# Where the sums of the down weights are made, and two small moves around the output projection, in a decoder layer on one core

## The chip, the cores and the metric

One Trainium2 chip, and one core of it. The metric is the device time of one execution of the whole layer in microseconds (us); lower is better. Several runs of a kernel are given as a median with the lowest and the highest. Engines are named as the profile names them: PE is the matrix engine (PEld its weight loads), DVE the vector engine, ACT the scalar engine, POOL the GpSimd engine. SP is the engine whose queue issues the DMA transfers of this kernel.

## The reference

One layer of a decoder with 1024 tokens of 1024 float32 values: one projection, two attention branches (a forgetting attention, and a sparse one that keeps 256 keys per query), a gated mix, and a SwiGLU feed-forward block, each of the last two behind a layer norm. Cut to what matters here:

```python
proj = x @ w_in[l]
(fq, fk, fv, f_logit, dq, dk, dv, iq, ik, iw, g_a, g_b) = _split_columns(proj)
o_a = _fox_attention(...)
o_b = _dsa_attention(...)
merged = (jax.nn.sigmoid(g_a) * (o_a @ w_branch_a[l])
          + jax.nn.sigmoid(g_b) * (o_b @ w_branch_b[l]))
x = _layer_norm(ALPHA * x + merged @ w_out[l], ln1_g[l], ln1_b[l])
gate, up = jnp.split(x @ w_ffn_in[l], 2, axis=-1)
ffn = (jax.nn.silu(gate) * up) @ w_ffn_out[l]
x = _layer_norm(ALPHA * x + ffn, ln2_g[l], ln2_b[l])
```

The feed-forward block is 1024 to 2 x 2816 and back to 1024.

## The kernel before, in words

Every float32 product is made of three matmuls on a high and a low part of each operand (`mm3`, lines 97 to 101): a weight tile is loaded, ACT copies it rounded (the high part), and POOL or DVE subtracts that from the original (the low part). PE cannot begin a product before its high part is there (line 99), nor go on past the first matmul before its low part is there (line 100).

The stages in order of time:

1. Projections and attention (to about 800 us). Between them PE works off "filler" projections, the last of which are the gates (`gate`, line 374): a product in a PSUM bank, a tanh on ACT (line 380), a write to DRAM (line 381). The PSUM pool of this stage is closed after the last gate, and the next stage takes its banks.
2. Branch projections (line 637 on). For each half of the tokens and each of four column groups, two branches: `load_wb` splits a branch weight (ACT line 631, POOL line 632 the first half of the low part, DVE line 633 the second half), PE makes two products of 12 matmuls each (24 in all), DVE folds the gate in. The buffers of the high and low parts are two deep. `load_wb` runs at raised priority. In the same loop, eight weights of the output projection are loaded and split: ACT line 671, POOL line 672, one instruction for all 1024 columns.
3. Output projection, layer norm and transposes (about 890 to 1022 us).
4. The up stage of the feed-forward block (line 829 on), 22 steps of 128 gate and 128 up columns. The products are made by Strassen's scheme (Winograd's form): seven products of 12 matmuls a step (five in the first three steps, whose other two were made ahead). For a step c, a gate weight `wraw` and an up weight `wup` are loaded, DVE makes four sums of them (lines 838 to 841, tiles `ss`), ACT and POOL split the seven into tiles `w` (lines 789 and 790), ten of which are in a ring. PE fills PSUM banks `pb`, eight deep; DVE empties each by adding it to running sums `u` and `h` (lines 806 and 858), ACT and DVE finish the gated product (lines 864, 866, 867).
5. The same step also prepares the weights of the next stage: a tile `wb` with four 128x256 blocks of `w_ffn_out` is loaded by two transfers (line 875), four sums are made in place (lines 877 to 880), each is written to a DRAM buffer `abd` (line 882). The other half of `abd` are the blocks of the gated product (line 889) and their sums (891 to 896).
6. The down stage (about 1465 us to the end) reads `abd` back and makes the seven products of 2816 to 1024.

The order on each engine is set at build time. PE's order in the stages 3 to 6 is written out by hand; the other engines' instructions are placed by a scheduler that takes, by priority, what its own model of the chip finds ready. Priority follows program order, and `high_priority(offset=HURRY)` raises it. A tile's buffer comes from a pool by its tag; a new tile of the tag waits until an old one is no longer used. So the scheduler starts a load as soon as its tag has a free buffer. Before the change:

```python
up = ffl.tile([128, 1024], F32, name="wup", tag="wup", bufs=2)
wb = ffl.tile([128, 4, 256], F32, name="wb", tag="wb", bufs=1)
```

The tag `wb` is used by the sums alone: as soon as the four writes of one step have landed, the tile of the next step is loaded, whatever step PE is at. Each engine, and SP's queue, works strictly in the order given to it: an instruction that waits holds up all behind it.

Of the kernel before, what the change touches and what calls it, by code (L numbers as in the profile page):

```python
# [8 lines left out]
F32 = mybir.dt.float32  # L9
# [3 lines left out]
AF = mybir.ActivationFunctionType  # L13
OP = mybir.AluOpType
# [24 lines left out]
AHEAD, LASTC, HURRY = 3, 8, 100  # L39
# [10 lines left out]
def trunk_kernel(ctx: ExitStack, tc: tile.TileContext, xT, xn, wt, wbr, wout, wfi, wfo,  # L50
                 lnp, bf, alq, alk, out):
    nc = tc.nc
    te, dve, act, pool, sp = nc.tensor, nc.vector, nc.scalar, nc.gpsimd, nc.sync
# [14 lines left out]
    def f(ap):  # L68
        return ap.bitcast(F32)
# [16 lines left out]
    def load_w(src, hi=None, lo=None):  # L86
        raw = wp.tile([128, 1024], F32, name="wraw", tag="wraw", bufs=2)
        sp.dma_start(raw, src)
        if hi is None:
            hi = wp.tile([128, 1024], F32R, name="whi", tag="whi", bufs=2)  # L90
            lo = wp.tile([128, 1024], F32R, name="wlo", tag="wlo", bufs=2)
        act.activation(hi, raw, AF.Copy)  # L92
        pool.tensor_tensor(lo, raw, f(hi), op=OP.subtract)  # L93
        return hi, lo
# [21 lines left out]
    def ps_mm():  # L116
        return psA.tile([128, 512], F32, name="mm", tag="mm", bufs=NMM)
# [52 lines left out]
    for h in range(2):  # L170
        s = slice(h * 512, h * 512 + 512)
        ps = ps_mm()
# [69 lines left out]
    for c in range(4):  # L242
        w = split_w(raw0, pool) if c == 0 else load_w(wt[C_IQ + c])
        iq = [idx.tile([128, 768], F32R, name="iq", tag="iq", bufs=4) for _ in range(2)]
        for q, (half, c0, n, d0) in enumerate(((0, 256, 256, 0), (1, 0, 512, 256))):
            ps = ps_mm()
# [6 lines left out]
        for a in range(2):  # L253
            h = 2 * c + a
            for i in range(2, 8):
                n = 128 * (i + 1)
# [109 lines left out]
    def proj_steps(ps, w, half):  # L366

        hi, lo = w
        for k in range(KT):
            mm3(ps, [(hi[:, k * 128:k * 128 + 128], lo[:, k * 128:k * 128 + 128],  # L370
                      XH[half][:, k], XL[half][:, k])], k == 0, k == KT - 1)
            yield

    def gate(br, c):
        w = load_w(wt[(C_GA, C_GB)[br] + c])
        for h in range(2):
            ps = ps_mm()
            yield from proj_steps(ps, w, h)
            g = at.tile([128, 512], F32, name="g", tag="g", bufs=2)
            act.activation(g, ps, AF.Tanh, scale=0.5)  # L380
            sp.dma_start(gdr[br][c, :, h * 512:h * 512 + 512], g)

    def project(br, pr, made):
# [220 lines left out]
    def ps_b():  # L604
        return psB.tile([128, 512], F32, name="ob", tag="ob", bufs=4)
# [6 lines left out]
    WOH, WOL = [], []  # L612
# [3 lines left out]
    def load_raw_b(src, shape):  # L616
        raw = bp.tile(shape, F32, name="braw", tag="braw", bufs=2)
        sp.dma_start(raw, src)
        return raw

    def load_o(o, br, s):

        for k in range(0, 4, 2):
            raw = load_raw_b(odr[br][k:k + 2, :, s].rearrange("k p t -> p k t"), [128, 2, 512])
            act.activation(o[:, 0, k:k + 2], raw, AF.Copy)
            dve.tensor_tensor(o[:, 1, k:k + 2], raw, f(o[:, 0, k:k + 2]), op=OP.subtract)
# [11 lines left out]
    for h in (1, 0):  # L638
        s = slice(h * 512, h * 512 + 512)
        if h:  # L640
            O = [xm.tile([128, 2, 4, 512], F32R, name=f"oh{br}", tag="x", bufs=4) for br in range(2)]
        else:
            O = [bp.tile([128, 2, 4, 512], F32R, name=f"ol{br}") for br in range(2)]
        MH[h] = xm.tile([128, KT, 512], F32R, name=f"mh{h}", tag="x", bufs=4)
        ML[h] = xm.tile([128, KT, 512], F32R, name=f"ml{h}", tag="x", bufs=4)
        load_o(O[0], 0, s)
        load_o(O[1], 1, s)
        for c2 in (range(4) if h else range(3, -1, -1)):
            m = []
            for br in range(2):  # L650
                if h or c2 < 3:
                    with tc.high_priority(offset=HURRY):
                        WB[br] = load_wb(br, c2)
                wh, wl = WB[br]
                for x in range(2):
                    c = 2 * c2 + x
                    g = bp.tile([128, 512], F32, name="g", tag="g", bufs=7)
                    sp.dma_start(g, gdr[br][c, :, s])
                    ps = ps_b()
                    mm3(ps, [(wh[:, b0:b0 + 128], wl[:, b0:b0 + 128], O[br][:, 0, k], O[br][:, 1, k])  # L660
                             for k, b0 in enumerate(range(x * 512, x * 512 + 512, 128))])
                    dve.scalar_tensor_tensor(g, g, 1.0, ps, op0=OP.add, op1=OP.mult)
                    m.append(g)
                    if br:
                        dve.tensor_tensor(g, g, m[x], op=OP.add)
                        act.activation(MH[h][:, c], g, AF.Copy, scale=0.5)
                        dve.scalar_tensor_tensor(ML[h][:, c], g, 0.5, f(MH[h][:, c]),
                                                 op0=OP.mult, op1=OP.subtract)
            k = c2 + 4 * (1 - h)
            raw = load_raw_b(wout[k * 128:k * 128 + 128], [128, 1024])  # L670
            act.activation(WOH[k], raw, AF.Copy)
            pool.tensor_tensor(WOL[k], raw, f(WOH[k]), op=OP.subtract)
    _bp.close()


# [76 lines left out]
    for t in range(NB):  # L752
        half, c0 = divmod(TOK[t] * 128, 512)
        bs = fin.tile([128, 2, 6], F32, name="bs", tag="bs", bufs=2)
        for n in range(2):
            ns = slice(n * 512, n * 512 + 512)
            ps = ps_b()
# [54 lines left out]
    for c in range(AHEAD):  # L812
        raw = load_raw(wfi[c])
# [9 lines left out]
    def ps_c():  # L823
        return psC.tile([128, 512], F32, name="pb", tag="pb", bufs=8)

    ffl, _ffl = open_pool("ffl")
    ring[0:0] = [(ffl, "wt0", 1)]
    ring += [(ffl, f"wt{k}", 1) for k in range(1, 4)]
    for c in range(FC):
        g = load_raw(wfi[c])  # L830
        up = ffl.tile([128, 1024], F32, name="wup", tag="wup", bufs=2)
        sp.dma_start(up, wfi[FC + c])
        g1_, g2_, u1_, u2_ = g[:, 0:512], g[:, 512:1024], up[:, 0:512], up[:, 512:1024]
        new = c >= len(ahead)
        a11, a12 = (slot(), slot()) if new else (None, None)
        s2, s3, s1, s4, a22 = (slot() for _ in range(5))
        r1, r2, r3, r4 = (ffl.tile([128, 512], F32, name="ss", tag="ss", bufs=4) for _ in range(4))
        dve.tensor_tensor(r1, u1_, u2_, op=OP.add)
        dve.tensor_tensor(r2, r1, g1_, op=OP.subtract)
        dve.tensor_tensor(r3, g1_, u1_, op=OP.subtract)  # L840
        dve.tensor_tensor(r4, g2_, r2, op=OP.subtract)
        if new:
            split(a11, g1_)
            split(a12, g2_)
        split(s2, r2)
        split(s3, r3)
        split(s1, r1)
        split(s4, r4)
        split(a22, u2_)
        u = c11(ps_c, (a11, a12)) if new else ahead[c]  # L850
        h = ffl.tile([128, 2, 512], F32, name="h", tag="h", bufs=3)
        U, sg, h0, h1 = u[:, 0], u[:, 1], h[:, 0], h[:, 1]

        def add(to, w, x, *more):
            ps = ps_c()
            product(ps, w, x)
            for o, i in ((to, to), *more) if to is not None else more:
                dve.tensor_tensor(o, ps, i, op=OP.add)  # L858

        add(U, s2, T2)  # L860
        add(None, s3, T3, (h0, U))
        add(None, s1, T1, (h1, h0), (U, U))
        add(U, s4, B22)
        act.activation(U, U, AF.Silu)
        add(h0, a22, T4)
        dve.tensor_tensor(h1, h1, U, op=OP.mult)
        dve.tensor_tensor(h0, h0, sg, op=OP.mult)


        j, x = divmod(c, 2)  # L870
        cols = slice(x * 256, x * 256 + 256)
        wb = ffl.tile([128, 4, 256], F32, name="wb", tag="wb", bufs=1)
        for y in range(2):
            rows = wfo[(2 * j + y) * 128:(2 * j + y + 1) * 128]
            sp.dma_start(wb[:, 2 * y:2 * y + 2], rows.rearrange("p (a n) -> p a n", a=2)[:, :, cols])
        b11, b12, b21, b22 = (wb[:, y] for y in range(4))
        dve.tensor_tensor(b11, b12, b11, op=OP.subtract)  # L877
        dve.tensor_tensor(b12, b22, b12, op=OP.subtract)  # L878
        dve.tensor_tensor(b22, b22, b11, op=OP.subtract)  # L879
        dve.tensor_tensor(b21, b21, b22, op=OP.subtract)  # L880
        for p, b in ((5, b11), (7, b12), (6, b22), (4, b21)):
            sp.dma_start(abd[p][j][:, 1, cols], b)
        if x == 0:
            even, even_u = h, U
            continue

        a11, a21, a12, a22 = even[:, 0], even[:, 1], h0, h1
        for p, a in ((1, a11), (2, a12), (4, a22)):
            sp.dma_start(abd[p][j][:, 0], a)
        q2, q3, q4 = U, sg, even_u  # L890
        dve.tensor_tensor(q3, a11, a21, op=OP.subtract)
        dve.tensor_tensor(a21, a21, a22, op=OP.add)
        dve.tensor_tensor(q2, a21, a11, op=OP.subtract)
        dve.tensor_tensor(q4, a12, q2, op=OP.subtract)
        for p, a in ((7, q3), (5, a21), (6, q2), (3, q4)):
            sp.dma_start(abd[p][j][:, 0], a)
# [166 lines left out]
```

## Time and profile before

| | us |
|---|---|
| median of 3 runs (lowest, highest) | 1687.06 (1686.71, 1687.7) |
| the profiled execution, its own time | 1685.55 |
| its span, first to last instruction | 1683.6 |
| PE busy | 1611.2 |
| DVE busy | 1186.1 |
| ACT busy | 777.3 |
| POOL busy | 673.3 |

All times of the trace are counted from the start of the span. A PE busy time is modelled and matmuls overlap, so a PE that is "busy" can still be slow; how fast it goes is read from the number of matmuls in a window. The granted clock is a share of 2.4 GHz. "Idle before, releaser" is the time an engine stood still before an instruction, and what ended that.

### The profile page before, as it was taken

The numbers are of one execution on the slowest core, as the hardware profiler recorded it, in microseconds if no ns is written. First come the engines' busy times: TensorE is split into PE (matmuls) and PEld (weight loads), VectorE is DVE, ScalarE is ACT, GpSimd is POOL, SyncE is SP. The second block draws the span as 40 slices with busy tenths as digits, with TensorE's granted clock in tenths as the row PEclk, the third lists the DMA queues.
The fourth block names the chain that finished last, engine by engine and source line by source line (L and its number), as shares of the span: only waits on it lengthen the run. The fifth ranks groups of instructions, "written<-read, shape, count | busy, mean of one in ns | idle before, by whom it ended". The sixth has DMA issues, their size and how long they took to land. (4 is left out here: it accounts for less than half of the span.)

```text
span 1683.6 us, 22519 instructions
## 1 busy us (share of the span) xinstructions
PE 1611.2 (96%) x7722; PEld 1314.1 (78%) x7722; DVE 1186.1 (70%) x2074; ACT 777.3 (46%) x1374; POOL 673.3 (40%) x652
## 2 busy tenths in 40 slices
PE   7998999998999999999999999999899999999997
PEld 5776887776788888888778877877677888888886
DVE  5889999979645454544775569776778766567776
ACT  6777878884444445544431034222123333253341
POOL 1122333332333333332441136434345555377673
PEclk9999999999999999999999999999899999999999
DMA  5112212121122222223865123565554333398552
GB/s 176 48 40 65 60 45 59 57 70 43 57 66 63 70 58 71 61 65 126 270 208 194 50 88 102 190 203 184 172 180 139 107 101 107 132 329 309 179 169 105
DMA packets 96379, 202.83 MB, mean 120 GB/s; under 512 B 10820, under 2 KB 37444, under 8 KB 96264
## 3 DMA queue, kind: packets, MB, share of 16 engines
q1 hardware_dynamic: 96264, 201.39, 36.6%
q8 instruction: 61, 1.00, 0.3%
q14 instruction: 54, 0.44, 0.1%
HBM read 139.40 MB, written 53.03 MB: 114 GB/s over the span
## 5 line engine op out<-in xcount | busy, mean ns | idle before, releaser
L99 PE MATMUL mm<-xh,whi 128*128 128x512 f32 (+1 forms) x720 | 296.0, 411 | 16.2 <-ACT whi L147 6.4
L101 PE MATMUL mm<-xl,whi 128*128 128x512 f32 (+1 forms) x720 | 281.4, 391 | 1.1 <-DVE xl L157 1.0
L100 PE MATMUL mm<-xh,wlo 128*128 128x512 f32 (+1 forms) x720 | 280.7, 390 | 0.5 <-DVE wlo L148 0.5
L479 POOL TENSOR_SCALAR p<-p,st 128x512 f32<-128x512 f32 (+1 forms) x192 | 113.8, 601 | 321.5 <-DVE st L476 268.8
L790 POOL TENSOR_TENSOR w<-ss,w 128x512 fp32r<-128x512 f32 x88 | 129.4, 1487 | 207.5 <-ACT w L789 188.8
L93 POOL TENSOR_TENSOR wlo<-wraw,whi 128x1024 fp32r<-128x1024 f32 x43 | 103.5, 2406 | 164.4 <-ACT whi L92 143.1
L99 PEld LDWEIGHTS mm<-xh,whi 128*128 128x128 f32 x720 | 136.8, 190 | 31.1 <-issue 6.4
L101 PEld LDWEIGHTS mm<-xl,whi 128*128 128x128 f32 x720 | 136.0, 189 | 32.0 <-DVE xl L157 2.3
L100 PEld LDWEIGHTS mm<-xh,wlo 128*128 128x128 f32 x720 | 136.8, 190 | 12.8 <-DVE wlo L148 1.0
L504 DVE TENSOR_TENSOR pl<-T,ph 128x512 fp32r<-128x512 f32 (+1 forms) x160 | 100.6, 634 | 36.6 <-ACT ph L503 34.7
L100 PE MATMUL acc<-fs 128*128 128x512 f32 x308 | 120.0, 389 | 0.6 <-DVE fs L930 0.6
L101 PE MATMUL acc<-fs 128*128 128x512 f32 x308 | 119.9, 389 | 0.0
L99 PE MATMUL acc<-fs 128*128 128x512 f32 x308 | 119.8, 389 | 0.0
L503 ACT ACTIVATE ph<-T 128x512 fp32r<-128x512 f32 (+1 forms) x160 | 87.3, 552 | 38.8 <-PE T L502 36.1
L310 ACT ACTIVATE junk<-sm,nt 128x1024 bf16<-128x1024 f32 (+2 forms) x93 | 96.8, 1041 | 14.6 <-DVE nt L318 12.8
L502 PE MATMUL T<-identf,p 128*128 128x128 f32 x576 | 90.6, 273 | 4.1 <-POOL p L479 2.0
L931 POOL TENSOR_TENSOR fs<-fraw,fs 128x512 fp32r<-128x512 f32 x47 | 81.1, 1740 | 26.9 <-ACT fs L929 23.1
L502 PEld LDWEIGHTS T<-identf,p 128*128 128x128 f32 x576 | 71.2, 140 | 26.1 <-DVE pl L504 4.1
L512 PE MATMUL O<-pl,V 128*128 128x256 f32 x320 | 82.3, 281 | 1.3 <-DVE pl L504 1.3
L511 PE MATMUL O<-ph,V 128*128 128x256 f32 x320 | 83.3, 282 | 0.0
L99 PE MATMUL pb<-x1h,w 128*128 128x512 f32 x176 | 72.0, 409 | 10.5 <-DVE h L858 9.3
L930 DVE TENSOR_TENSOR fs<-fraw,fs 128x512 fp32r<-128x512 f32 x47 | 57.0, 1225 | 31.1 <-ACT fs L929 31.1
(284 smaller groups left out, 4167.6 us busy)
## 6 DMA issues: line engine op xcount, KB each, us to landing
wraw<-in_wt_dram SPq DMA_DIRECT2D x45, 512.0 KB
fraw<-abd SPq DMA_DIRECT2D x30, 512.0 KB
wraw<-in_wfi_dram SPq DMA_DIRECT2D x25, 512.0 KB
wup<-in_wfi_dram SPq DMA_DIRECT2D x22, 512.0 KB
wb<-in_wfo_dram SPq DMA_DIRECT2D x44, 256.0 KB
abd<-wb SPq DMA_DIRECT2D x88, 128.0 KB
abd<-h SPq DMA_DIRECT2D x44, 256.0 KB
abd<-u SPq DMA_DIRECT2D x33, 256.0 KB
```

Source lines behind the costliest of these rows:

```text
L93: pool.tensor_tensor(lo, raw, f(hi), op=OP.subtract)
L99: te.matmul(ps, ah, bh, start=(first and i == 0), stop=False)
L100: te.matmul(ps, al, bh, start=False, stop=False)
L101: te.matmul(ps, ah, bl, start=False, stop=(last and i == n - 1))
L310: act.activation(j[:, :128 * (i + 1)], SM[i], AF.Sign, bias=bias(x), accum_out=s[:, x:x + 1])
L479: pool.tensor_scalar(pc, pc, st[:, 3:4], 1.0, op0=OP.mult, op1=OP.mult)
L502: te.transpose(T[:, s * 128:s * 128 + 128], P[qq][:, j * 128:j * 128 + 128], identf)
L503: act.activation(ph[:, c:], T[:, c:], AF.Copy)
L504: dve.tensor_tensor(pl[:, c:], T[:, c:], f(ph[:, c:]), op=OP.subtract)
L511: te.matmul(O, V[:, j, :], ph[:, r0:r0 + 256], start=(j == 0), stop=False)
L512: te.matmul(O, V[:, j, :], pl[:, r0:r0 + 256], start=False, stop=(last and jj == 1))
L790: pool.tensor_tensor(s[:, 1], raw, f(s[:, 0]), op=OP.subtract)
```

## The change

Three edits. The sums of `wb` go from DVE to POOL, and `wb` shares the tag, and so the buffers, of `wup`, three instead of two and one (the memory is the same). The tanh of the very last gate gets raised priority. The low part of each output weight is made by two instructions of 512 columns instead of one of 1024.

```diff
@@ gate
-            act.activation(g, ps, AF.Tanh, scale=0.5)
+            if (br, c) == (1, 7):
+                with tc.high_priority(offset=HURRY):
+                    act.activation(g, ps, AF.Tanh, scale=0.5)
+            else:
+                act.activation(g, ps, AF.Tanh, scale=0.5)
@@ branch projections
-            pool.tensor_tensor(WOL[k], raw, f(WOH[k]), op=OP.subtract)
+            for a in (slice(0, 512), slice(512, 1024)):
+                pool.tensor_tensor(WOL[k][:, a], raw[:, a], f(WOH[k][:, a]), op=OP.subtract)
@@ up stage
-        up = ffl.tile([128, 1024], F32, name="wup", tag="wup", bufs=2)
+        up = ffl.tile([128, 1024], F32, name="wup", tag="wup", bufs=3)
@@ up stage, sums of the down weights
-        wb = ffl.tile([128, 4, 256], F32, name="wb", tag="wb", bufs=1)
+        wb = ffl.tile([128, 1024], F32, name="wb", tag="wup", bufs=3).rearrange("p (a n) -> p a n", a=4)
...
-        dve.tensor_tensor(b11, b12, b11, op=OP.subtract)
-        dve.tensor_tensor(b12, b22, b12, op=OP.subtract)
-        dve.tensor_tensor(b22, b22, b11, op=OP.subtract)
-        dve.tensor_tensor(b21, b21, b22, op=OP.subtract)
+        pool.tensor_tensor(b11, b12, b11, op=OP.subtract)
+        pool.tensor_tensor(b12, b22, b12, op=OP.subtract)
+        pool.tensor_tensor(b22, b22, b11, op=OP.subtract)
+        pool.tensor_tensor(b21, b21, b22, op=OP.subtract)
```

PE's order is the same before and after. The line numbers of the changed kernel are 2 higher at the raised tanh (380 becomes 382), 4 higher between the two first edits (631, 632 and 671 become 635, 636 and 675), and 5 higher from the second edit on (672 becomes 677, 790 becomes 795, 858 becomes 863, 877 to 880 become 882 to 885).

**ACT at the end of the attention stage.** `g<-mm` is the last gate's tanh, `oh` are attention outputs, `whi` is a branch weight. Before:

```order
L526 ACTIVATE o<-O 64x256
L625 ACTIVATE oh_8480<-braw 128x1024
L631 ACTIVATE whi<-wraw 128x1024
L380 ACTIVATE g<-mm 128x512
L625 ACTIVATE oh_8480<-braw 128x1024
```

Now:

```order
L530 ACTIVATE o<-O 64x256
L629 ACTIVATE oh_8480<-braw 128x1024
L382 ACTIVATE g<-mm 128x512
L635 ACTIVATE whi<-wraw 128x1024
L629 ACTIVATE oh_8480<-braw 128x1024
```

The tanh has moved ahead of one split of a branch weight.

**POOL in the branch projections.** `wlo` is half of a branch weight's low part, `wol` the low part of an output weight. Before:

```order
L672 TENSOR_TENSOR wol_8470<-braw,woh_8469 128x1024
L632 TENSOR_TENSOR wlo<-wraw,whi 128x512 x3
L672 TENSOR_TENSOR wol_8478<-braw,woh_8477 128x1024
L632 TENSOR_TENSOR wlo<-wraw,whi 128x512
L672 TENSOR_TENSOR wol_8476<-braw,woh_8475 128x1024
```

Now:

```order
L677 TENSOR_TENSOR wol_8470<-braw,woh_8469 128x512 x2
L636 TENSOR_TENSOR wlo<-wraw,whi 128x512 x4
L677 TENSOR_TENSOR wol_8478<-braw,woh_8477 128x512 x2
L677 TENSOR_TENSOR wol_8476<-braw,woh_8475 128x512 x2
```

The eighth branch weight's low part (the fourth `wlo` here) no longer stands behind the fifth output weight's; elsewhere both halves of each output weight stand together, where the one instruction stood. On ACT the eighth `whi` has likewise moved ahead of the fifth `woh`.

**DVE and POOL in the middle of the up stage.** DVE before: `u` and `h` rows that read `pb` empty a PSUM bank, `wb` rows are the sums.

```order
L877 TENSOR_TENSOR wb<-wb 128x256
L878 TENSOR_TENSOR wb<-wb 128x256
L879 TENSOR_TENSOR wb<-wb 128x256
L858 TENSOR_TENSOR h<-pb,u 128x512
L880 TENSOR_TENSOR wb<-wb 128x256
L858 TENSOR_TENSOR h<-pb,h 128x512
L858 TENSOR_TENSOR u<-pb,u 128x512 x2
```

POOL now, one step of the repeating pattern:

```order
L795 TENSOR_TENSOR w<-wup,w 128x512
L795 TENSOR_TENSOR w<-wraw,w 128x512
L882 TENSOR_TENSOR wb<-wb 128x256
L883 TENSOR_TENSOR wb<-wb 128x256
L884 TENSOR_TENSOR wb<-wb 128x256
L885 TENSOR_TENSOR wb<-wb 128x256
L795 TENSOR_TENSOR w<-wraw,w 128x512
L795 TENSOR_TENSOR w<-ss,w 128x512 x4
```

DVE has no `wb` row any more and is otherwise in the old order but for a few neighbours. On POOL the four sums stand once a step, between the first and the second split of a gate weight; the `wb` in them belongs to the step after that gate weight's. On SP a `wb` load stands behind the writes of the gated product of an earlier step, and is no longer free to run ahead of them.

## Rows read from the trace of the kernel before

**Rows 1.** The page: its first line and part 1 (busy time, share, instructions).

```profile
span 1683.6 us, 22519 instructions
...
PE 1611.2 (96%) x7722; PEld 1314.1 (78%) x7722; DVE 1186.1 (70%) x2074; ACT 777.3 (46%) x1374; POOL 673.3 (40%) x652
```

**Rows 2.** Windows, up stage: PE, PEld, DVE, ACT, POOL busy (instructions), clock, DMA, GB/s.

```profile
1022.09:1040.00 17.91, 15.24 (x60) 12.01 (x59) 17.73 (x17) 6.18 (x12) 16.62 (x11) 0.90 0.52 170
...
1080.00:1280.00 200.00, 183.34 (x747) 143.93 (x746) 146.73 (x204) 45.87 (x85) 86.52 (x62) 0.96 0.55 176
1280.00:1460.00 180.00, 180.00 (x781) 146.43 (x780) 120.33 (x147) 57.66 (x95) 94.35 (x66) 1.00 0.33 113
```

**Rows 3.** Windows, instructions on `ob` alone (branch products): PE, PEld, DVE, ACT.

```profile
800.50:850.00 49.50, 43.25 (x174) 34.41 (x175) 9.30 (x14) 0.00 (x0) 0.94 0.79 260
```

**Rows 4.** Waits of PE: us in total, times, longest.

```profile
PE pb L99 <- DVE h L858: 9.3, 4, 3.1
...
PE pb L99 <- DVE u L858: 5.5, 6, 3.4
PE ob L100 <- POOL wlo L632: 4.0, 3, 2.7
PE ob L99 <- ACT g L380: 2.7, 1, 2.7
PE pb L100 <- POOL w L790: 2.7, 1, 2.7
```

**Rows 5.** Waits of DVE in 1080 to 1280 us.

```profile
DVE wb L877 <- DMA wb<-in_wfo_dram: 38.2, 13, 4.2
```

**Rows 6.** Timeline of DVE: start, us, instruction, [idle before, releaser].

```profile
1180.98 0.68 DVE L858 TENSOR_TENSOR u<-pb,u 128x512 f32<-128x512 f32 x1
1184.27 1.55 DVE L877 TENSOR_TENSOR wb<-wb 128x256 f32<-128x256 f32 x1 [2.60 <-DMA wb<-in_wfo_dram]
...
1188.67 0.68 DVE L858 TENSOR_TENSOR h<-pb,u 128x512 f32<-128x512 f32 x1
```

**Rows 7.** Timeline of PE: four of its waits.

```profile
802.76 0.62 PE L99 MATMUL ob<-oh,whi 128*128 128x512 f32 x1 [2.72 <-ACT g L380]
...
847.83 0.80 PE L100 MATMUL ob<-oh,wlo 128*128 128x512 f32 x1 [2.68 <-POOL wlo L632]
...
1025.16 0.80 PE L100 MATMUL pb<-t2h,w 128*128 128x512 f32 x1 [2.67 <-POOL w L790]
...
1189.50 0.77 PE L99 MATMUL pb<-x1h,w 128*128 128x512 f32 x1 [3.11 <-DVE h L858]
```

**Rows 8.** The chain that ended last, in order of time: start, us, what.

```profile
1148.96 4.71 DMA wb<-in_wfo_dram
...
1181.22 2.93 DMA wb<-in_wfo_dram
```

**Rows 9.** Durations: tile `wb` and line 672 (ns min/median/max), POOL in 1280 to 1460 us (us, mean ns).

```profile
L877 DVE TENSOR_TENSOR wb<-wb x22: 416/426/1549, 1023.1 to 1263.2; 128x256 f32<-128x256 f32 x22
...
L672 POOL TENSOR_TENSOR wol<-braw,woh x8: 2378/2412/2859, 808.5 to 857.5; 128x1024 fp32r<-128x1024 f32 x8
...
L790 POOL TENSOR_TENSOR w<-ss,w 128x512 fp32r<-128x512 f32 x36 | 53.2, 1484 | 51.2 <-ACT w L789 44.1 <-DVE h L858 6.0 <-DVE u L894 0.6
...
L790 POOL TENSOR_TENSOR w<-wup,w 128x512 fp32r<-128x512 f32 x9 | 11.6, 1294 | 5.9 <-ACT w L789 5.9
```

**Rows 10.** Timeline of POOL, around two of PE's waits.

```profile
843.73 2.38 POOL L672 TENSOR_TENSOR wol<-braw,woh 128x1024 fp32r<-128x1024 f32 x1 [4.92 <-ACT woh L671]
846.06 1.72 POOL L632 TENSOR_TENSOR wlo<-wraw,whi 128x512 fp32r<-128x512 f32 x1
...
1020.67 1.35 POOL L790 TENSOR_TENSOR w<-ss,w 128x512 fp32r<-128x512 f32 x1 [25.48 <-ACT w L789]
1021.98 1.72 POOL L790 TENSOR_TENSOR w<-wup,w 128x512 fp32r<-128x512 f32 x1
1023.65 4.55 POOL L790 TENSOR_TENSOR w<-ss,w 128x512 fp32r<-128x512 f32 x3
```

**Rows 11.** Timeline of ACT, at the last tanh and at the eighth branch weight.

```profile
801.05 1.04 ACT L631 ACTIVATE whi<-wraw 128x1024 fp32r<-128x1024 f32 x1
802.11 0.60 ACT L380 ACTIVATE g<-mm 128x512 f32<-128x512 f32 x1
...
843.56 1.04 ACT L631 ACTIVATE whi<-wraw 128x1024 fp32r<-128x1024 f32 x1
```

## Prediction

> **What bounds the kernel now.** I read the page first: PE is busy for 96% of the span [rows 1], so only a stretch in which PE stands or crawls has anything to give. Next the windows, where the number of matmuls tells how fast PE goes. From 1280 to 1460 us it makes 781 in 180 us, one per 0.2305 us, without a pause; this is the same stage and the same tiles as 1080 to 1280 us, where only 747 fit into 200 us [rows 2]. At the later rate those take 747 x 0.2305 = 172.2 us, so **27.8 us are lost there**. The granted clock in that stretch is 0.96, a mix of mostly 2.4 GHz and some 1.2 GHz: part of the loss is standing, part the slow matmuls behind each stand.
>
> Why PE stands there is in its waits: the longest are for line 858, DVE emptying PSUM banks [rows 4], 3.11 us at 1189.50 for one [rows 7]. There are eight banks and a product of 12 matmuls takes 12 x 0.2305 = 2.77 us, so DVE must have been about 22 us late. What made it late is in DVE's own waits: 38.2 us of those 200 it stood before line 877, for a `wb` load [rows 5]; with 146.73 us busy [rows 2] that leaves almost nothing. The timeline shows one case: an emptying at 1180.98, then 2.60 us of waiting for the load, then sums, and the next emptying only at 1188.67 [rows 6]. The chain that ended last runs through the same loads, 2.93 to 4.71 us each [rows 8]. So in this stretch DVE's order is paced by a single-buffered DRAM round trip whose result nobody reads before the down stage.
>
> Two smaller places: the start of the up stage, where PE waits 2.67 us for a low part from POOL [rows 4, 7], and the branch projections, where 174 matmuls took 49.5 us [rows 3]; at 0.2305 us they are 40.1, so 9.4 are lost: 2.7 for the tanh, 4.0 for POOL's low parts [rows 4], and the remaining 2.7 in slow matmuls, granted clock 0.94 [rows 3].
>
> **The change, part by part.**
>
> *The sums leave DVE.* Their waits for DMA go with them, since no `wb` row is left in DVE's order. DVE keeps work like that of 1280 to 1460 us, 120.33 busy of 180 [rows 2], a stretch in which no sum ran and PE lost nothing. Taken whole: **-27.8**. Bounds: 0 (DVE is late for another reason) and -27.8.
>
> *POOL gets 88 sums of 128x256.* Nothing in the trace shows one there. Lower bound: a 128x1024 subtraction takes 2.412 us and a 128x512 one 1.294 [rows 9], a slope of 1.118 per 512 columns, so 1.294 - 0.559 = 0.73 us. Upper bound: 1.48, a 128x512 split among DVE's work [rows 9]. I take 0.73, since the width is what differs. A step is 7 x 2.77 = 19.4 us, 180 us hold 9.3 of them, 37 sums: 27 to 55 us on top of 94.35 [rows 2], so POOL is at 67 to 83% of the stretch and keeps up. The ring of ten split tiles gives it 10 x 2.77 = 27.7 us of lead over PE, which is the cover for this item; without the cover it would cost its full length.
>
> A rule speaks against this item. The rows show first that a sum on DVE takes 0.426 us as a median but up to 1.549 [rows 9], and a split on POOL 1.48 in the mean where an undisturbed one takes 1.29 [rows 9]: the two slow each other. The Trainium skill (Perfetto Trace Analysis, section Optimizing Scalar/DVE Operations) says that GpSimd and DVE share an SBUF read port, so that moving operations from one to the other might not help. The rows agree with the sharing; by the rule the gain would be that of rival A below instead of the 27.8.
>
> *A later start.* At the head of the up stage POOL makes a split, a split of `wup`, and then the one PE waits for [rows 10]. The new order puts one sum between them: +0.73 on the 2.67 us wait, **+0.9** with some of DVE's interference; bounds 0 and +1.5.
>
> *The first steps are tight.* In the first three steps a step is only 5 x 2.77 = 13.9 us, and sums and loads of three `wb` stand among the splits. POOL's low part for PE's first wait comes at about 1025.2 + 0.9 = 1026.1. Behind it stand 7 splits and 6 sums (10.4 + 4.4 us), so about 1041; only then does SP, which stands before the last sum's write, issue the loads of the third step, up to 4.71 us each [rows 8] and one behind the other, 1047; then 4 sums and 2 splits (5.9 us): the low part of the third step's first product is there at about 1053. PE needs it at 1026.1 + 1.4 (slow matmuls) + 10 x 2.77 = 1055.2. DVE's sums `ss` wait for the same loads, with 22 us of banks as cover. Covered, but barely: I set **+2**, bounds 0 and +10 (three waits like 2.67, each with its slow matmuls). From the fourth step on a step has 19.4 us and POOL some 13.4 us of work, so the lead grows.
>
> *Loads.* SP now issues a `wb` load behind writes of the gated product of a step about four earlier. Its sums stand in POOL's order ahead of a split that PE needs more than a step later, so a load of 4.71 us plus sums of 3 us fits into 19.4 us. Bytes are the same, spread over the stage: no cost.
>
> *The tanh.* PE's first branch product waits for the bank that the tanh frees [rows 7]. The tanh now runs ahead of a 1.04 us split [rows 11]: **-1.0**. That split belongs to the second branch weight, 24 matmuls or 5.5 us later, so its delay of 0.5 us is covered. What is late next is POOL: PE comes 1 us earlier to low parts that stand behind output weights. Bounds 0 and -2.4 (the slow matmuls go too).
>
> *The pieces.* Two halves with nothing between them are no faster, (2 x 1.294 against 2.412: +0.18 us each, covered). What counts is that the eighth branch weight's low part passes an output weight's: at 843.73 POOL began 2.38 us of `wol`, and PE waited until 847.83 for the `wlo` behind it [rows 7, 10], whose `whi` was made from 843.56 on [rows 11] behind a `woh`. Both step aside: the 2.7 us wait goes, and half of the 2.7 us of slow matmuls with it, **-4.0**; bounds 0 and -5.4 (the other two waits of line 632 too).
>
> *Sum.* -27.8 + 0.9 + 2.0 - 1.0 - 4.0 = -29.9. From the profiled execution's 1685.55 that gives 1655.65; the median of the runs stands 1.5 above that execution, so 1657.2, said as **1657**.
>
> **The rivals.**
>
> A. *The shared work of DVE and POOL keeps half the loss.* DVE's additions with both inputs in SBUF (`ss`, `h`, and the sums of `u`) still slow down whenever POOL works, and POOL now works more. For it: 1.549 against 0.426 [rows 9]. Against it: in 1280 to 1460 us both worked side by side, 120.33 and 94.35 of 180, and PE lost nothing [rows 2]. Half of 27.8 kept: 1657 + 13.9 = 1671.
>
> B. *POOL takes over the wait, and it is slower.* POOL is in order too. If a `wb` load lands later than POOL arrives at the sums by more than the ring's lead of 27.7 us, the split behind them is late, and PE pays in every step: a wait of about 2.7 and 1.35 of slow matmuls, 4 us, in 19 steps 77, less 33 of gains: 1687 + 44 = 1731. Against it: the lead, and loads of under 5 us [rows 8].
>
> C. *The loads are not paced in fact.* If the shared tag let `wb` still run ahead, it would crowd out `wup`, DVE would wait for `ss`, and the stretch would lose what it loses now: about 1682, the small moves alone. Against it: SP's order has one `wb` load a step to the end of the stage.
>
> **How the numbers follow.** The forecast has 0.76, A 0.12, B 0.05, C 0.07. The forecast's own range: at the low end all three bounds at their best, 1687.06 - 27.8 - 2.4 - 5.4 = 1651.5, and 1650 for an up stage with no early wait at all; at the high end the early steps at +10 and no gain in the branch projections, 1687.06 - 27.8 + 0.9 + 10 = 1670. That is nearly A, so the range is 1650 to 1671. Some 0.2% (3.4 us) is what a measurement of this kernel can tell from no change. The forecast, A and most of C are faster than that: 0.93; 0.03 for C's end near no change; 0.04 slower, from B.
>
> **What would show it.** Right: in the up stage PE's waits for the emptying are gone and the window of 200 us that is now at 747 holds over 850 matmuls; DVE waits nowhere for `wb`, POOL briefly; the sums take 0.7 to 1.0 us on POOL; DMA runs evenly to the end of the stage; PE's first wait in the stage is 3 to 4 us; the tanh wait is about 1.7 us, and the 2.68 us wait is gone. Wrong: waits of PE for POOL's low parts throughout the stage (B), for the emptying (A), or in the first three steps by more than 5 us.

## The result and the profile after

The changed kernel takes **1663.92 us** (median; 1662.34 to 1665.01), the kernel before 1686.97 beside it: a ratio of 0.986, 95% interval 0.9848 to 0.9872, so 23 us faster. The forecast was 1657, a gain of 29.9 us, with a range of 1650 to 1671. The profiled execution after takes 1662.34 us with a span of 1660.5.

The start of the first matmul of each stage tells where the 23.1 us of span came from. The first output-projection matmul starts at 894.36 instead of 898.09 us (-3.7), the stage behind it has its 124.0 us in both, the up stage takes 420.7 instead of 442.6 (-21.9), and from the first down product to the end of the span it is 221.4 instead of 218.9 (+2.5).

The busy times of the page, and all engines in the 200 us that [rows 2] show for before (total, PE, PE's weight loads, DVE, ACT, POOL, clock, DMA share, GB/s):

```profile
PE 1601.0 (96%) x7722; PEld 1309.5 (79%) x7722; DVE 1139.2 (69%) x1986; ACT 772.6 (47%) x1374; POOL 749.9 (45%) x748
```

```profile
1080.00:1280.00 200.00, 198.14 (x856) 160.20 (x855) 132.31 (x155) 56.62 (x105) 136.27 (x113) 1.00 0.48 158
```

856 matmuls stand where 747 stood, DVE has less to do and POOL more. PE's waits (total us, times, longest), against [rows 4]:

```profile
PE ob L100 <- POOL wlo L636: 4.6, 3, 3.3
PE pb L100 <- POOL w L795: 3.7, 1, 3.7
PE pb L99 <- DVE u L811: 1.9, 3, 1.0
...
PE ob L99 <- ACT g L382: 1.3, 1, 1.3
PE pb L99 <- DVE h L863: 1.1, 1, 1.1
```

The longest wait for the emptying of banks, 3.4 us before [rows 4], is down to 1.1 us and is gone after 1160 us. Two places got worse: the start of the up stage, where PE waits 3.7 instead of 2.7 us, and the fourth branch weight's low part, for which PE did not wait before. In PE's timeline they read so (start, us, instruction, [idle before, releaser]); the last row is one of the small waits for the emptying:

```profile
821.28 0.50 PE L100 MATMUL ob<-oh,wlo 128*128 128x512 f32 x1 [3.29 <-POOL wlo L636]
...
1022.43 0.80 PE L100 MATMUL pb<-t2h,w 128*128 128x512 f32 x1 [3.69 <-POOL w L795]
...
1114.15 0.50 PE L99 MATMUL pb<-t2h,w 128*128 128x512 f32 x1 [1.01 <-DVE u L811]
```

The sums' durations on POOL (ns min/median/max) and the longest waits of DVE and POOL from 1040 to 1460 us:

```profile
L882 POOL TENSOR_TENSOR wb<-wb x22: 729/740/749, 1011.6 to 1392.6; 128x256 f32<-128x256 f32 x22
L883 POOL TENSOR_TENSOR wb<-wb x22: 729/1074/1197, 1018.2 to 1393.4; 128x256 f32<-128x256 f32 x22
L884 POOL TENSOR_TENSOR wb<-wb x22: 729/1241/1251, 1022.3 to 1394.5; 128x256 f32<-128x256 f32 x22
```

```profile
DVE ss L843 <- POOL w L795: 71.5, 18, 5.7
```

```profile
POOL wb L882 <- DMA wb<-in_wfo_dram: 34.0, 14, 6.1
```

DVE no longer waits for `wb`; POOL does, 34 us in all, and DVE stands behind POOL instead, because its `ss` buffers come free when POOL has split them. The first of a step's four sums now starts for the last time at 1392.6 us, before at 1263.2 [rows 9]: the sums are spread over the stage. The change did two things to them, and the profile cannot tell which of the two paid.

### The profile page after: what moved, and what is told of

Its sections match the earlier page's. It is cut to its first block, busy times and chain, and to the rows that moved or that the text cites. A ratio compares the mean times of both kernels' runs of the same rounds, so it can differ in the third digit from the quotient of the medians.

```text
span 1660.5 us, 22523 instructions
## 1 busy us (share of the span) xinstructions
PE 1601.0 (96%) x7722; PEld 1309.5 (79%) x7722; DVE 1139.2 (69%) x1986; ACT 772.6 (47%) x1374; POOL 749.9 (45%) x748
## 5 line engine op out<-in xcount | busy, mean ns | idle before, releaser
L795 POOL TENSOR_TENSOR w<-ss,w 128x512 fp32r<-128x512 f32 x88 | 121.9, 1404 | 73.4 <-ACT w L794 73.4
L310 ACT ACTIVATE junk<-sm,nt 128x1024 bf16<-128x1024 f32 (+2 forms) x93 | 96.8, 1040 | 14.5 <-DVE nt L318 12.6
L812 ACT ACTIVATE u<-u 128x512 f32<-128x512 f32 x22 | 13.9, 632 | 168.2 <-DVE u L811 168.2
L843 DVE TENSOR_TENSOR ss<-wup 128x512 f32<-128x512 f32 x22 | 34.4, 1565 | 83.4 <-POOL w L795 71.5
```

Source lines behind the costliest of these rows:

```text
L310: act.activation(j[:, :128 * (i + 1)], SM[i], AF.Sign, bias=bias(x), accum_out=s[:, x:x + 1])
L795: pool.tensor_tensor(s[:, 1], raw, f(s[:, 0]), op=OP.subtract)
```

## The experiments

Stages in us, from the profiled executions: start of the first output-projection matmul; up stage; first down product to the end of the span; then the median time, and the 95% interval of its ratio to the kernel before. That kernel was run again beside each group of runs, with medians of 1686.65 to 1687.71.

| kernel | start | up stage | down | median | ratio |
|---|---|---|---|---|---|
| before | 898.1 | 442.6 | 218.9 | 1686.97 | |
| changed | 894.4 | 420.7 | 221.4 | 1663.92 | 0.9848 to 0.9872 |
| up stage's edit alone | 899.1 | 420.7 | 219.8 | 1664.19 | 0.985 to 0.9882 |
| shared ring alone | 898.5 | 414.6 | 218.9 | 1658.72 | 0.9814 to 0.9854 |
| sums on POOL alone | 896.5 | 458.6 | 218.4 | 1700.36 | 1.0063 to 1.0094 |
| half buffers, no pacing | 899.0 | 438.7 | 218.6 | 1682.54 | 0.995 to 0.9978 |
| ring, POOL from step 5 | 898.5 | 415.8 | 219.6 | 1659.85 | 0.9814 to 0.9843 |
| tanh and pieces alone | 899.2 | 442.0 | 220.2 | 1685.36 | 0.9978 to 0.9999 |
| ring, tanh | 895.5 | 414.5 | 219.3 | 1654.68 | 0.9789 to 0.9818 |
| ring, tanh, pieces | 897.3 | 414.5 | 220.3 | 1657.66 | 0.9815 to 0.9842 |
| ring, tanh, low parts half on DVE | 893.0 | 414.6 | 218.7 | 1651.61 | 0.9767 to 0.9797 |
| the same, first split on DVE | 892.4 | 413.8 | 219.7 | 1650.06 | 0.9772 to 0.9799 |

The first column also tells what one execution is worth: the six kernels in which that code is untouched reach it at 896.5 to 899.1. The stage between that start and the up stage has the same code in all; it takes 122.4 us in three of the profiled executions (up stage's edit alone, POOL from step 5, first split on DVE) and 123.8 to 124.0 in the others.

**The up stage's edit alone.** The diff without its tanh and without its pieces.

> Kernel before with the up stage's edit alone (sums on POOL, shared ring of three); tanh and output-weight splits as before. Theory, that the edits are independent and the up stage carries the gain: the up stage keeps its 21.2 us and the down stage its 1.8 us loss, so 19.4 us under the kernel before (ratio 0.9885); branch projections back at 98.4 us up to their last product; first wait of the up stage 3.7 us as in the changed kernel. Rival, that the small edits decide how the up stage starts: a gain of under 16 or over 22 us and another first wait.

The up stage takes 420.7 us as in the changed kernel, with a first wait of 3.68 us, and the median is the same to 0.3 us. What follows the first wait differs: PE waits 2.24 us for the emptying at 1077.84 where it waited 1.14 in the changed kernel, and has fewer slow matmuls. (The 21.2 and 1.8 us in the expectation were read from a matmul 0.7 us too late; 21.9 and 2.5 are right.) The up stage carries the gain, and its length does not hang on the two small edits.

**The shared ring alone.** The sums stay on DVE.

```diff
-        up = ffl.tile([128, 1024], F32, name="wup", tag="wup", bufs=2)
+        up = ffl.tile([128, 1024], F32, name="wup", tag="wup", bufs=3)
...
-        wb = ffl.tile([128, 4, 256], F32, name="wb", tag="wb", bufs=1)
+        wb = ffl.tile([128, 1024], F32, name="wb", tag="wup", bufs=3).rearrange("p (a n) -> p a n", a=4)
```

> Kernel before with the shared ring of three alone; the sums stay on DVE. Theory, that DVE was late because it stood in order before a load that had one buffer: with the load issued a step ahead its waits for wb between 1080 and 1280 us fall from 38.2 to under 10 us and PE's waits for the emptying go, so 12 to 21 us under the kernel before; DVE carries 1.7 us more work a step than in the changed kernel and still has a third of its time free. Rival, that the engine decides (sums on DVE are late whenever they are loaded): waits of PE for the emptying stay, gain under 5 us.

28.0 us of the up stage, more than the whole change gave. All engines in two stretches, DVE's waits of 1080 to 1280 us against [rows 5], and the first and last start of the sums:

```profile
1080.00:1280.00 200.00, 200.00 (x868) 162.75 (x867) 159.70 (x207) 58.58 (x107) 109.00 (x76) 1.00 0.52 166
1280.00:1460.00 180.00, 180.00 (x783) 146.71 (x782) 128.01 (x157) 57.03 (x87) 88.77 (x61) 1.00 0.49 155
```

```profile
DVE wb L877 <- DMA wb<-in_wfo_dram: 12.1, 10, 3.9
DVE h L866 <- ACT u L864: 7.0, 10, 0.7
DVE wb L878 <- DMA wb<-in_wfo_dram: 3.1, 10, 0.7
```

```profile
L877 DVE TENSOR_TENSOR wb<-wb x22: 412/426/1427, 1023.5 to 1377.6; 128x256 f32<-128x256 f32 x22
```

PE stands nowhere in the up stage but at its start, with DVE busier (159.70) than before (146.73). DVE still stands 15.2 us before `wb`, not under 10 as expected, and it costs nothing: the sums run to 1377.6 instead of 1263.2 us, so their waits are thinner and none makes DVE 22 us late.

**The sums on POOL alone.** Here `wb` keeps its one buffer.

```diff
-        dve.tensor_tensor(b11, b12, b11, op=OP.subtract)
+        pool.tensor_tensor(b11, b12, b11, op=OP.subtract)
...
```

> Kernel before with the sums moved to POOL alone; wb keeps its one buffer and wup its two. Theory, that the engine with a lead over PE can stand where DVE can't: POOL waits 2 to 5 us before each sum's load, 40 us or more in all, PE's waits for the emptying go, gain 10 to 21 us. Rival, that POOL takes over the wait (loads that run ahead and are not paced): PE waits for POOL's low parts in many steps, gain under 5 us or a loss.

This kernel is slower by 13 us; the up stage loses 16.0. PE's nine waits for the emptying are 27 us in all. The rows of one case, from POOL's, DVE's and PE's timelines:

```profile
1107.69 0.74 POOL L877 TENSOR_TENSOR wb<-wb 128x256 f32<-128x256 f32 x1 [3.22 <-DMA wb<-in_wfo_dram]
...
1111.97 4.18 POOL L790 TENSOR_TENSOR w<-ss,w 128x512 fp32r<-128x512 f32 x3
```

```profile
1113.30 1.73 DVE L838 TENSOR_TENSOR ss<-wup 128x512 f32<-128x512 f32 x1 [9.97 <-POOL w L790]
```

```profile
1120.13 0.79 PE L99 MATMUL pb<-t2h,w 128*128 128x512 f32 x1 [6.83 <-DVE u L806]
```

POOL stands for the load, four sums and a split follow, and only the next split frees the buffer for which DVE stood 9.97 us; the emptying comes after it in DVE's order, and PE waits 6.83 us. So both theories missed the place: POOL does take over the wait, as the rival said, and the price is paid through DVE's emptying, not at POOL's low parts.

**Half a buffer more, no pacing.** Each `wb` as two half tiles in a ring of three halves of their own.

```diff
-        wb = ffl.tile([128, 4, 256], F32, name="wb", tag="wb", bufs=1)
+        wb = [ffl.tile([128, 2, 256], F32, name="wb", tag="wb", bufs=3) for _ in range(2)]
...
```

> Kernel before with each wb made as two half tiles in a ring of three halves of their own (half a buffer more, no tie to wup); sums on DVE. Theory pacing, that the loss comes from sums that run ahead of the stage and cluster before 1280 us: they cluster as before or earlier, the waits of DVE for wb remain in part, gain under 10 us. Rival buffering, that one buffer too few was the whole cause: gain of 15 us or more without any pacing, close to the shared ring's 28.

The up stage is 3.9 us shorter. The waits only move to the second half's load, and the sums end even earlier, at 1223 us:

```profile
DVE wb L878 <- DMA wb<-in_wfo_dram: 29.4, 16, 3.5
```

```profile
L878 DVE TENSOR_TENSOR wb<-wb x22: 411/472/1508, 1026.4 to 1223.2; 128x256 f32<-128x256 f32 x22
```

Half a buffer more does not return the loss, while the shared ring, which also spreads the sums over the stage, returns all of it. That speaks for the pacing. A second whole buffer without pacing was not tried, so how much of the ring's gain is the pacing and how much the second buffer is not shown.

**The ring, with POOL from the fifth step on.**

```diff
+        eng = dve if c < 4 else pool
-        dve.tensor_tensor(b11, b12, b11, op=OP.subtract)
+        eng.tensor_tensor(b11, b12, b11, op=OP.subtract)
...
```

> Kernel before with the shared ring of three; the sums of the first four steps on DVE, the other eighteen on POOL. Theory, that the move to POOL costs its 6 us in the first steps, where sums stand among the splits PE is about to need: first wait of the up stage 2.67 us, no further wait there, up stage 414 to 417 us, time within 2 us of the shared ring with DVE alone (1658.7). Rival, that POOL's work slows DVE's throughout: up stage 419 us or more, 1663 or more.

It came out as the first theory had it, but for one wait of 1.1 us for the emptying: against the ring alone, eighteen steps' sums on POOL cost 1.2 us, so the other 4.9 go with the first four. A slowing by the two engines' shared work through the whole stage is not the price.

That slowing is seen all the same, and in the changed kernel it is part of one wait. Ahead of PE's wait at 1078.94 us there, six instructions of DVE that touch no PSUM bank took 8.28 us in all, while POOL worked almost without a break (1067.6 to 1077.6). With the ring alone, where POOL stood from 1070.6 to 1079.3, the same six took 5.17 us; in this run 7.19. The emptying behind them begins at 1078.11 in the changed kernel, and at 1076.20 in this run, where PE does not wait: the six began 0.8 us earlier and took 1.1 us less. The rows are two of the six, and the emptying behind them, in the changed kernel; then PE's wait there; then the same two with the ring alone:

```profile
1074.71 1.78 DVE L846 TENSOR_TENSOR ss<-wraw,ss 128x512 f32<-128x512 f32 x1
1076.41 1.78 DVE L899 TENSOR_TENSOR u<-h,u 128x512 f32<-128x512 f32 x1
1078.11 0.68 DVE L863 TENSOR_TENSOR h<-pb,u 128x512 f32<-128x512 f32 x1
```

```profile
1078.94 0.47 PE L99 MATMUL pb<-x1h,w 128*128 128x512 f32 x1 [1.14 <-DVE h L863]
```

```profile
1072.89 0.68 DVE L841 TENSOR_TENSOR ss<-wraw,ss 128x512 f32<-128x512 f32 x1
...
1074.43 0.68 DVE L894 TENSOR_TENSOR u<-h,u 128x512 f32<-128x512 f32 x1
```

An emptying, which reads PSUM, took 0.68 us beside POOL's work too (at 1073.00 us in the changed kernel).

**Tanh and pieces alone.**

> Kernel before with the tanh at higher priority and the output weights' low parts in two pieces; up stage as before. Theory, that these are worth what the stage account of the changed kernel shows: 3.5 us under the kernel before (ratio 0.998), with the new wait of 3.3 us for the fourth branch weight's low part. Rival, that the new wait comes from elsewhere (loads of the up stage): no wait of over 1 us at that place and 5 us or more gained.

The gain is 1.7 us in the median, with an interval that nearly reaches no change. The new wait is there and longer. PE after it, and what POOL did ahead of it:

```profile
822.21 0.79 PE L100 MATMUL ob<-oh,wlo 128*128 128x512 f32 x1 [3.95 <-POOL wlo L636]
822.80 0.63 PE L101 MATMUL ob<-oh,whi 128*128 128x512 f32 x1
823.23 0.63 PE L99 MATMUL ob<-oh,whi 128*128 128x512 f32 x1
```

```profile
814.10 6.37 POOL L677 TENSOR_TENSOR wol<-braw,woh 128x512 fp32r<-128x512 f32 x4 [2.38 <-ACT woh L675]
820.43 1.73 POOL L636 TENSOR_TENSOR wlo<-wraw,whi 128x512 fp32r<-128x512 f32 x1
```

Four pieces of two output weights, 6.37 us, stand ahead of the low part that PE wants.

**The ring and the tanh, in one piece.** This is the diff without its pieces, and with the sums on DVE.

> Kernel before with the shared ring of three (sums on DVE) and the tanh at higher priority; output weights split in one piece. Theory, that the tanh alone moves the eighth branch weight's low part ahead of the output weight's, so the 2.68 us wait goes without any pieces, and that PE then waits for the fourth: less than the 3.3 and 3.95 us seen with pieces, since four pieces took 6.37 us where two whole ones took 5.24. 1656 to 1658.5. Rival, that the pieces are what removes the wait: the 2.68 us wait stays, time as with the shared ring alone less 0.5 to 1.

The median, 1654.68, is 1.3 us under the range expected. The 2.68 us wait of [rows 7] is gone without any pieces: the tanh alone puts the eighth branch weight's low part (843.13) ahead of the output weight's (844.54) on POOL. For the fourth PE waits 1.74 us.

```profile
815.51 2.59 POOL L676 TENSOR_TENSOR wol<-braw,woh 128x1024 fp32r<-128x1024 f32 x1 [0.23 <-DMA g<-gdr]
818.06 1.72 POOL L636 TENSOR_TENSOR wlo<-wraw,whi 128x512 fp32r<-128x512 f32 x1
...
843.13 1.45 POOL L636 TENSOR_TENSOR wlo<-wraw,whi 128x512 fp32r<-128x512 f32 x1 [4.98 <-ACT whi L635]
844.54 2.85 POOL L676 TENSOR_TENSOR wol<-braw,woh 128x1024 fp32r<-128x1024 f32 x1
```

**The ring, the tanh and the pieces.** This is the changed kernel with its sums back on DVE.

> The changed kernel with its sums of the down weights back on DVE (shared ring of three, tanh and pieces kept). Theory, that moving the sums to POOL costs 6 us in the up stage and the pieces give nothing: 4 to 9 us under the changed kernel (1655 to 1660), and not under the same kernel without pieces (1654.7), with the wait for the fourth branch weight at 3 us or more against 1.74 there. Rival, that the pieces are worth some of the 4 us that the prediction gave them: 1651 to 1653.5, fourth wait under 1.7 us.

The time is 6.3 us under the changed kernel, and the up stage 6.2 us shorter, so the move to POOL cost that. It is 3.0 us over the kernel without pieces, though the two intervals overlap a little (0.9815 to 0.9818). The wait for the fourth branch weight is 1.98 here, not 3 or more as expected: it varies between executions of kernels that have the same code there (3.29, 3.95, 1.98).

**Low parts half on DVE.** This is the kernel with ring and tanh, and each output weight's low part in two pieces, the second of them on DVE in the first half of the branch projections:

```diff
-            pool.tensor_tensor(WOL[k], raw, f(WOH[k]), op=OP.subtract)
+            for e, a in ((pool, slice(0, 512)), (dve if h else pool, slice(512, 1024))):
+                e.tensor_tensor(WOL[k][:, a], raw[:, a], f(WOH[k][:, a]), op=OP.subtract)
```

> As the run with the shared ring and the tanh, but each output weight's low part of the first half of the branch projections is made half on POOL and half on DVE (in the second half two pieces on POOL). Theory, that the fourth branch weight waits behind 5 to 6 us of output weights on POOL: with 2.6 us instead its wait goes, another 2 to 4 us, 1653 to 1656, the best so far. Rival, that DVE's halves delay the emptying of the banks or the branch weights' second halves, made on DVE: a wait of PE for DVE in the branch projections, no gain over the tanh alone.

The median, 1651.61, is 1.4 us under the range expected. POOL has two halves ahead of the fourth low part instead of four, and it is there at 816.59 + 1.74 us:

```profile
813.12 3.51 POOL L677 TENSOR_TENSOR wol<-braw,woh 128x512 fp32r<-128x512 f32 x2 [2.12 <-ACT woh L675]
816.59 1.74 POOL L636 TENSOR_TENSOR wlo<-wraw,whi 128x512 fp32r<-128x512 f32 x1
```

PE's wait for it is gone; this code reaches the output projection 5 us before that of the kernel before.

**The first split on DVE.** One more edit to that kernel: in the first step `s2`'s low part, behind two splits on POOL, is made on DVE, and the two sums and the ACT copy that it needs get raised priority with it.

```diff
+            if c == 0:
+                act.activation(s2[:, 0], r2, AF.Copy)
+                dve.tensor_tensor(s2[:, 1], r2, f(s2[:, 0]), op=OP.subtract)
...
-        split(s2, r2)
+        if c:
+            split(s2, r2)
```

> The fastest run so far (shared ring with DVE, tanh, output weights half on DVE: 1651.6) with one more edit: the low part of the up stage's first split of a sum is made on DVE, ahead of the other sums, so that it doesn't stand behind two splits on POOL. Theory, that the 2.67 us wait there is that queue's: it falls to about 1 us and the slow matmuls behind it go in part, 1648.5 to 1650.5. Rival, that the wait moves on to the next split, or that DVE is late with the emptying: no gain, another wait within the first three products.

The wait falls to 1.81 us, not to 1, the slow matmuls behind it stay, and the up stage is 0.8 us shorter. The median, 1650.06, is the lowest of all, but its interval overlaps that of the run above. In the profiled executions 1.6 us lie in the stage ahead of the up stage (122.4 against 124.0), which the edit does not touch. So this last step is seen in the profile but not in the times.

## Why the prediction was right, and where it was wrong

The time is inside the range and on the forecast side; the gain is 6.8 us short. That it lies in the range is in part luck: the change held the ring beside the move, and the forecast gave the ring's worth to the move, which by itself makes the kernel 13 us slower. By its own steps:

- **The bound, right.** The loss between 1080 and 1280 us is DVE's order paced by a load nobody needs yet. Its size, 27.8 us, is almost what the shared ring alone returns: 28.0 over the stage, and 868 matmuls instead of 747 in those 200 us, 27.9 at 0.2305 each.
- **"The sums leave DVE", -27.8: the size right, the cause wrong.** This is the step that failed. It put the whole gain on the move to the other engine and costed the ring, under "Loads", at nothing. The runs show the reverse: ring alone -28.0 us in the up stage, move alone +16.0, both -21.9. I read "DVE waits for `wb`" as "the work must leave DVE"; the same rows said that the last step's sums began at 1263.2 us, with 201 us of the stage to go [rows 9]. That the loads ran so far ahead was the thing to mend.
- **The rule I argued against came out.** The Trainium skill (Perfetto Trace Analysis, section Optimizing Scalar/DVE Operations) says that moving operations between GpSimd and DVE might not help. Here the move costs 6.1 us behind the ring (420.7 against 414.6) and 16.0 without it. A port no run here shows; that DVE is slower beside POOL they do (8.28 against 5.17 us above). Over the whole stage that slowing is worth little: with the first four steps on DVE the move costs 1.2 us.
- **Start and first steps, +0.9 and +2: inside the bounds, sized too small, and put in the wrong place.** Together they are 6.1, against the ring alone. The first wait is 1.0 us longer, as forecast; some five more slow matmuls, 0.427 instead of 0.2305 us apart, are 1.0; the waits of 1.14, 0.55, 1.01 and 0.30 us up to 1160 are 3.0; 1.1 is not placed. The forecast looked for POOL's low parts to be late in the first three steps. Those end at 1066 us, and PE waits in them only at the start. Behind them, where "the lead grows" was written, it was DVE that was late: it stood for the buffers of `ss` that POOL had yet to split, and was slowed beside POOL. The 22 us of banks did not cover it. (The upper bound, +10 for three waits, is 12 at the price of 4 us that the prediction itself takes under B.)
- **POOL's price, 0.73 us:** right as the least; two of the four sums have medians of 1.07 and 1.24 us. Its loads were to make POOL wait "briefly"; it waits 34.0 us, up to 6.1 at once.
- **The tanh, -1.0:** its wait is 1.30 us here and 1.76 to 2.05 in the other kernels that have it, against 2.72 [rows 7] (2.1 to 2.9 in those without it). The size is right within that spread, but the tanh did more: it also moved the eighth low part ahead.
- **The pieces, -4.0: wrong.** The 2.68 us wait goes with the tanh. The pieces, forecast at +0.18 us each, add 1.1 us for two output weights (6.37 against 5.24 in the kernel before) at a place whose cover, PE's late arrival, the tanh had just taken away. "What is late next is POOL" was written beside the tanh, and then not put into the sum. In the kernels with pieces on POOL alone PE also waits for a later low part, at about 862 to 865 us (0.97, 2.00 and 2.32), where the kernel before has no wait. Tanh and pieces were to give 5.0, and up to the output projection 3.7 were gained in the profiled execution. Part of that is chance: in the three kernels that have this code the output projection starts at 894.4, 897.3 and 899.2 us.
- **The down stage, 0 forecast, +2.5.** 1.4 of it are small waits for the split tiles. The other kernels have 218.4 to 220.3 here, without an order that goes with their edits; it stays open what of this is the change's.
- **Rivals.** A (shared work of the two engines), as a loss kept through the whole stage, falls with the fifth run above; its slowing is seen, and is part of one wait. B (POOL takes over the wait, slower) is true of the move without the ring, 1700.36 us, and its path is DVE's emptying. C (no pacing) did not occur; the half buffers, with the sums on DVE, are the nearest to it, and their up stage keeps 438.7 of the 442.6 us.

## What to carry to other kernels

When an engine stands for a load in its own order, ask first why the load is asked for then: tying its buffer to the ring of the stage's own loads cost no memory here and gave all of the loss back, while moving the work to an engine that feeds the first one carried the wait along and made it longer. What the receiving engine frees for the first one, and how much the two slow each other, belongs into the price. Where a change has two parts, price each without the other. And when a wait is taken off, price at once the cover that its lateness gave to the next queue.

## What the runs showed of the chip that was not expected

PE's clock did not follow the length of a wait. After the 3.95 us of the kernel with tanh and pieces alone (822.21 above) the granted clock is 0.50, so 1.2 of 2.4 GHz, for eleven matmuls 0.427 us apart; after the 3.29 us at the same place of the changed kernel it stays at 1.00. All engines in a stretch behind each wait, the first kernel's and then the changed one's:

```profile
822.80:826.80 4.00, 4.00 (x11) 3.12 (x10) 1.14 (x1) 0.00 (x0) 3.51 (x3) 0.50 0.90 265
```

```profile
821.60:825.60 4.00, 4.00 (x19) 3.25 (x18) 2.54 (x3) 0.27 (x1) 3.83 (x3) 1.00 0.82 262
```

The head of the up stage shows the same. Behind the 3.69 us of the changed kernel, and behind the 3.68 us of the kernel with the up stage's edit alone:

```profile
1023.30:1027.00 3.70, 3.70 (x10) 2.84 (x10) 2.52 (x3) 1.00 (x2) 3.70 (x3) 0.50 0.42 141
```

```profile
1026.50:1030.00 3.50, 3.50 (x17) 2.82 (x16) 2.31 (x3) 0.81 (x2) 3.50 (x3) 1.00 0.44 142
```

And in the fastest kernel a wait of 1.81 us at 1016.98 is followed by a clock of 0.50. Ahead of the 3.95 us PE had stood 1.94 us at 801.41, ahead of the 3.29 us it had stood 1.30 at 801.12; whether that decides is not shown. So one stand of PE here costs its length, or its length and some 2 us more (eleven matmuls, 0.197 each), and a forecast should keep both ends.
